# Tiles cut to the token group, and attention queries ahead of delta queries, in a two-layer streaming encoder

## The chip, the cores and the metric

The kernel runs on one core of a Trainium2 chip. The metric is the device time of one execution in microseconds. A kernel is timed in several runs; one further execution is profiled, and every row below comes from it.

## The reference

One inference step over two layers for 2048 prompt tokens and 8 x 16 sample tokens, model width 1024, float32. Cut to what matters:

```python
# layer 0
z = rms_norm(h) @ w_in        # a_q a_k a_v a_g | b_q b_k b_v b_g b_beta b_alpha
# mixer A: 8 query heads, 2 key heads of 64; a query block of 64 sees its chunk and two before
o_a = softmax([q k^T / 8 - slope * dist, sink]) v          # q, k rms-normed per head
# mixer B: 4 heads of 128; conv of width 4 + SiLU on q, k, v; l2-normed q, k
a_mat = tril(beta k k^T * decay, -1) + I                   # per block of tokens
u, w = solve(a_mat, [beta v, beta k exp(G)])
for each block:                                            # recurrence over blocks
    v_new = u - w S;  o = q_dec S + (q k^T * decay) v_new
    S = S * g_tot + k_dec^T v_new
y = h + concat(o_a * silu(a_g), rms_norm(o_b) * silu(b_g)) @ w_out
# layer 1: projection to u and gate, trailing means over 2/4/8/16 minus u, group map, gate, out
```

## The kernel before

The 2176 tokens are worked in four groups: group 0 has four prompt blocks of 128 and the sample block (n = 640 columns), groups 1 to 3 have four prompt blocks (n = 512). Within a group both layers run to the end. A projection is three matmuls for each of eight input tiles (high and low float32r halves: `XH`, `XL`, weights `wh`, `wl`). `proj_fm` (L682 to L684) puts features on partitions, `tok_major` (L1246 to L1248) tokens, `out_half` (L717 to L719) makes the output projections. Weights come in the order of `weight_plan`: in group 0 as float32, split on ScalarE, VectorE and GpSimd (L453, L457) and stored; in later groups loaded as split pairs (`wk` to `w`). Loads are asked for two blocks ahead on SyncE's queue.

The heads come in two pairs. For a pair, `b_keys` projects and convolves two delta keys and, for each head, `system` builds the decay table (`decay_logs`: L854 on VectorE, L855 on GpSimd; `decay_exp`: L864 on TensorE), takes k k^T (L898) and forms `L`. After the second head `b_chain` begins: `b_inverse` inverts the 32 x 32 diagonal blocks in 31 steps of two VectorE instructions (L963, L964), sends them through DRAM (`Xd`), and joins them with small matmuls (L990 to L1025); `b_recur` runs the recurrence (L1130, L1147, L1158), in group 0 also over the sample's states (L1177, L1181, L1202). `b_queries` projects and convolves two delta queries and two values (taps: L840; tanh product: L845). `a_queries` projects attention queries, normalises them and transposes them (L1348, L1354); then `a_attend` does the banded softmax (L1406, L1410, L1420, L1424, L1435 to L1437), in group 0 also for the sample (`unit_s`). `conv` evacuates PSUM with ScalarE into one of two `cb` buffers (L820). After both pairs come the gate projections, the two halves of the output projection, and layer 1.

The program text is put out by a planner. The projections call `tick` with their own price; `start`ed jobs (generators such as `b_chain`, `a_attend`, `rest` of a convolution) are stepped when their planned time has come. The framework then orders each engine's instructions by this priority as they become ready in its own model.

Large tiles live in 17 shared slots: eleven wide ones of 1280 elements per partition and six narrow ones of 1024. `slot` gives a tile of up to 1024 elements a narrow slot if one is free, else a wide one, in the order in which slots were dropped; a larger tile takes a wide one alone. With none free it steps the planner forward until one is dropped:

```python
        while True:
            if size <= SMALL and free_small:
                tag = free_small.pop(0)
                break
            if free_big:
                tag = free_big.pop(0)
                break
            if not progress():
```

A tile in a reused slot waits for the last reader of the tile that was there. Before the change the tiles of a pair (`kT`, `L`, `D`, queries, values `vb`, attention output `A`, gates, splits) have the width of group 0 (2 x 640 elements) in every group, and so has the decay table.

Of the kernel before, what the change touches and what calls it, by code (L numbers as in the profile page):

```python
# [90 lines left out]
def weight_plan():  # L91
# [5 lines left out]
    def add(part, cut):  # L97
        plan.append((part, cut))
# [27 lines left out]
    def queries(pr):  # L126
        for o in (0, 1024):
            for h in (2 * pr, 2 * pr + 1):
                add("B", cols("in", span(C_B + o + P * h, P)))
        c = np.concatenate([span(C_Q + 256 * g + P * pr, P) for g in range(2)])  # L130
        for k in range(2):
            add("A", k_half("in", 4 * k, c))

    for k in range(2):
        add("A", k_half("in", 4 * k, np.concatenate([span(C_K, 256), span(C_BA, 8)])))
    for pr in range(2):
        keys(pr)
        queries(pr)
    for pr in range(2):
# [86 lines left out]
def hybrid_kernel(  # L226
# [433 lines left out]
    def group(gix, norm_job):  # L660
# [189 lines left out]
        def decay_logs(h):  # L850

            r = slot([P, 2, NBMAX, P], F32R)
            rh, rl = r[:, 0], r[:, 1]
# [4 lines left out]
        def decay_exp(r, d):  # L858

            for b0, b1 in banks:  # L860
                pe = psum("sc")
                w = P * (b1 - b0)
                for i in range(2):
                    mm(pe[:, 0:w], m_le_r, r[:, i, b0:b1, :].rearrange("p c i -> p (c i)"),  # L864
                       start=(i == 0), stop=(i == 1))
                S.activation(d[:, P * b0:P * b1], pe[:, 0:w], AF.Exp)
            drop(r)
# [79 lines left out]
        def b_inverse(pr):  # L947
# [25 lines left out]
            XT = slot([P, 2 * NBMAX, P])  # L973
            G.memset(XT[:, 0:nh, :].rearrange("p c i -> p (c i)"), 0.0)
            XA = slot([P, 2 * NBMAX, 64])
# [9 lines left out]
            ta = slot([P, 2 * NBMAX, 32])  # L985
# [25 lines left out]
            ta = slot([64, 2 * NBMAX, 64])  # L1011
# [21 lines left out]
        def b_queries(pr):  # L1033
            kT, L, b1s, nb2s = st["k", pr]
            qas, ssqs = [], []
            vb = slot([P, 2, TMAX])
            st["q", pr] = (qas, ssqs, vb)

            def scores(e):
                qt, at = qas[e][:, 0, 0:n], qas[e][:, 1, 0:n]  # L1040
# [49 lines left out]
            for e in range(2):  # L1090
                qas.append(slot([P, 2, TMAX]))
                ssqs.append(buf([P, NBMAX], "ssq", 4))
                for _ in conv(2 * pr + e, qas[e][:, 0, 0:n], scores(e)):
                    pass
# [4 lines left out]
        def b_recur(pr):  # L1099
            kT, L, b1s, nb2s = st["k", pr]  # L1100
            qas, ssqs, vb = st["q", pr]
# [39 lines left out]
            for c in range(npb):  # L1141
                kds, rq, pv_ = [], [], []
                for e in range(2):
# [4 lines left out]
                    mm(p1[:, P:2 * P], qas[e][:, 0, tk], Sst[2 * pr + e], start=True, stop=True)  # L1148
# [6 lines left out]
                for e in range(2):  # L1155
# [3 lines left out]
                    mm(p2[:, P:2 * P], qas[e][:, 1, P * c:P * c + P], vn, start=True, stop=True)  # L1159
# [7 lines left out]
            if samp:  # L1167
                c = npb
                for e in range(2):
                    h = 2 * pr + e  # L1170
                    yield from room(4)
                    sin = slot([P, NBAT, P])
# [4 lines left out]
                    V.tensor_copy(kq[:, :, 1, :], qas[e][:, 0, srow].rearrange("p (b i) -> p b i", i=DSEQ))  # L1177
# [5 lines left out]
                    sx = slot([P, 2, NBAT, DSEQ])  # L1183
# [603 lines left out]
```

## Time and profile before

| | us |
|---|---|
| median of 3 runs | 1970.59 (1967.81 to 1972.84) |
| profiled execution | 1969.22 |
| its span | 1967.3 |
| TensorE busy | 1859.4 |
| VectorE busy | 1249.1 |

The span runs from the first to the last instruction of the profiled execution; the rest of its time, 1.9 us, lies around it. Busy times are sums over the engine's instructions; matmuls overlap each other, and the busy time counts a moment once. The granted clock is the mean over a stretch, as a share of 2.4 GHz.

### The profile page before, as it was taken

Reading aid. Unit: us, or ns where it says so; the run is one execution under the profiler, and the core shown is the slowest. Engines: PE = TensorE matmul, PEld = TensorE weight load, DVE = VectorE, ACT = ScalarE, POOL = GpSimd, SP = SyncE. Lnnn points to the kernel's source line nnn. Section 1 sums busy time; section 2 is a strip of 40 time slices with the busy share of each in tenths; the row PEclk is TensorE's granted clock in tenths of the full one; section 3 lists DMA queues with packets and bytes.
Section 4 is the critical chain, followed back from the end, with each engine's and each line's share of the span. In section 5 each row is a group of like instructions: output and inputs, shape, how many; then the busy total and the mean of one; then the engine's idle time right before and its main releaser. Section 6 shows DMA issues by size and latency. Waiting matters only on the chain.

```text
span 1967.3 us, 34503 instructions
## 1 busy us (share of the span) xinstructions
PE 1859.4 (95%) x12994; PEld 1689.5 (86%) x12994; DVE 1249.1 (63%) x3439; ACT 759.6 (39%) x1954; POOL 492.3 (25%) x628
## 2 busy tenths in 40 slices
PE   5989977999999999899999999999999999999999
PEld 4888876998999888789889888789889888889889
DVE  5897795546564586954445597954445587854343
ACT  5446445324332345551312346551322346451210
POOL 4561350332433331401101332301102332210000
PEclk8999997999999999999999999999999999999999
DMA  6343342565668542244457643344566543344454
GB/s 263 120 169 115 121 166 71 196 223 176 230 223 286 207 162 89 97 154 172 161 194 267 217 155 97 110 141 150 184 223 257 199 140 97 127 142 170 166 194 182
DMA packets 93875, 335.13 MB, mean 170 GB/s; under 512 B 35805, under 2 KB 44253, under 8 KB 64269
## 3 DMA queue, kind: packets, MB, share of 16 engines
q1 hardware_dynamic: 93708, 332.92, 48.5%
q8 instruction: 103, 1.69, 0.3%
q14 instruction: 64, 0.52, 0.1%
HBM read 254.31 MB, written 78.58 MB: 169 GB/s over the span
## 4 chain that ended last, share of the span: by engine, by line
PE 66%; DVE 15%; DMA 3%; issue 2%; ACT 2%; POOL 2%; SPq 0%; DVEq 0%; POOLq 0%; ACTq 0%
PE pj L682 11%; PE pj L683 10%; PE pj L684 10%; PE pj L717 6%; PE pj L718 6%; PE pj L719 6%; DVE A L964 3%; DVE tm L963 3%; DVE B L840 2%; DVE A L1354 1%; PE tp L1420 1%; DMA w<-wk 1%; PE sc L1735 1%; PE rc L1130 1%; PE sc L1736 1%
## 5 line engine op out<-in xcount | busy, mean ns | idle before, releaser
L682 PE MATMUL pj<-XH,w 128*128 128x512 f32 (+3 forms) x1488 | 541.6, 364 | 4.4 <-ACT cb L820 2.1
L684 PE MATMUL pj<-XH,w 128*128 128x512 f32 (+3 forms) x1488 | 534.1, 359 | 0.3 <-POOL w L457 0.3
L683 PE MATMUL pj<-XL,w 128*128 128x512 f32 (+3 forms) x1488 | 532.7, 358 | 0.0
L682 PEld LDWEIGHTS pj<-XH,w 128*128 128x128 f32 x1488 | 282.2, 190 | 36.0 <-ACT cb L820 3.2
L717 PE MATMUL pj<-w,B 128*128 128x256 f32 x1088 | 308.8, 284 | 2.6 <-DVE A L723 2.6
L684 PEld LDWEIGHTS pj<-XH,w 128*128 128x128 f32 x1488 | 282.2, 190 | 31.5 <-POOL w L457 0.6
L718 PE MATMUL pj<-w,B 128*128 128x256 f32 x1088 | 307.7, 283 | 1.5 <-POOL w L457 1.5
L683 PEld LDWEIGHTS pj<-XL,w 128*128 128x128 f32 x1488 | 282.4, 190 | 29.3 <-issue 0.7
L719 PE MATMUL pj<-w,B 128*128 128x256 f32 x1088 | 306.4, 282 | 0.0
L723 DVE TENSOR_TENSOR A<-pj,A 128x256 f32<-128x256 f32 x272 | 114.9, 422 | 179.5 <-PE pj L719 179.2
L717 PEld LDWEIGHTS pj<-w,B 128*128 128x128 f32 x1088 | 206.4, 190 | 3.7 <-DVE A L723 3.2
L718 PEld LDWEIGHTS pj<-w,B 128*128 128x128 f32 x1088 | 206.0, 189 | 1.9 <-POOL w L457 1.7
L719 PEld LDWEIGHTS pj<-w,B 128*128 128x128 f32 x1088 | 207.3, 191 | 0.0
L457 POOL TENSOR_TENSOR w<-wst,w 128x640 fp32r<-128x640 f32 (+3 forms) x60 | 111.1, 1854 | 127.2 <-ACT w L453 117.4
L840 DVE SCALAR_TENSOR_TENSOR B<-cb,taps,B 128x512 f32<-128x512 f32 x144 | 122.1, 851 | 11.7 <-ACT B L829 10.5
L1246 PE MATMUL pj<-w,XH 128*128 128x256 f32 (+1 forms) x368 | 108.9, 296 | 5.5 <-DMA w<-wk 5.5
L703 POOL TENSOR_TENSOR B<-B,B 128x512 fp32r<-128x512 f32 (+1 forms) x32 | 44.4, 1386 | 256.7 <-ACT B L702 139.5
L1248 PE MATMUL pj<-w,XL 128*128 128x256 f32 (+1 forms) x368 | 107.2, 291 | 0.0
L1247 PE MATMUL pj<-w,XH 128*128 128x256 f32 (+1 forms) x368 | 107.2, 291 | 0.0
L695 DVE SCALAR_TENSOR_TENSOR B<-B,pj 128x512 f32<-128x512 f32 (+1 forms) x60 | 36.3, 606 | 98.2 <-ACT B L694 97.8
L964 DVE TENSOR_TENSOR A<-A,tm 32x112 f32<-32x112 f32 (+27 forms) x248 | 95.2, 384 | 5.2
L963 DVE TENSOR_TENSOR tm<-A,A 32x112 f32<-32x112 f32 (+27 forms) x248 | 93.0, 375 | 7.1 <-DMA A<-Ld 2.0
(338 smaller groups left out, 3627.1 us busy)
## 6 DMA issues: line engine op xcount, KB each, us to landing
w<-wk SPq DMA_DIRECT2D x168, 1024.0 KB, 4.8
wk<-w SPq DMA_DIRECT2D x56, 1024.0 KB, 6.6
wst<-in_wts SPq DMA_DIRECT2D x56, 512.0 KB, 4.4
A<-in_x SPq DMA_DIRECT2D x31, 512.0 KB, 4.6
out_y<-A SPq DMA_DIRECT2D x17, 512.0 KB, 3.0
w<-wk SPq DMA_DIRECT2D x6, 1056.0 KB, 6.0
B<-in_xt SPq DMA_DIRECT2D x12, 512.0 KB, 4.7
w<-wk SPq DMA_DIRECT2D x12, 512.0 KB, 3.3
```

The lines of the kernel that those rows point to most:

```text
L457: eng.tensor_tensor(lo[:, a:b], st[:, a:b], f32(hi[:, a:b]), op=ALU.subtract)
L682: mm(pp[:, 0:w], wh[:, k, :], xh[:, k, t0:t1], start=(k == 0), stop=False)
L683: mm(pp[:, 0:w], wh[:, k, :], xl[:, k, t0:t1], start=False, stop=False)
L684: mm(pp[:, 0:w], wl[:, k, :], xh[:, k, t0:t1], start=False, stop=(k == KT - 1))
L717: mm(pp[:, 0:256], oh[:, tk], wh[:, k, :], start=(k == 0), stop=False)
L718: mm(pp[:, 0:256], oh[:, tk], wl[:, k, :], start=False, stop=False)
L719: mm(pp[:, 0:256], ol[:, tk], wh[:, k, :], start=False, stop=(k == 3))
L723: V.tensor_tensor(ysl, pp[:, 0:256], ysl, op=ALU.add)
L840: V.scalar_tensor_tensor(dst[:, 0:Tp], cb[:, j:j + Tp], taps[:, m, j:j + 1], dst[:, 0:Tp], op0=ALU.mult, op1=ALU.add)
L963: V.tensor_tensor(t3, bc(Lb[:, j + 1:32, j], w), bcm(Xb[:, j, 0:w], r), op=ALU.mult)
L964: V.tensor_tensor(Xb[:, j + 1:32, 0:w], Xb[:, j + 1:32, 0:w], t3, op=ALU.subtract)
L1246: mm(pp[:, 0:N], xh[:, k, tk], wh[:, k % 4, :], start=(k == 0), stop=False)
```

## The change

Shared tiles get the width of their group (`n` for `TMAX`, `nb` for `NBMAX`). The decay table becomes two tiles, one for each half. In the weight plan and in the program the attention queries of pair 0 come before its delta queries; pair 1 keeps its order. In group 0 the sample's attention queries are kept in the sample columns and the first 256 columns of the attention output tile, which is taken in `a_queries`. A delta query's two halves may take two narrow slots. The sample recurrence takes both its tiles at once when two slots are free; before it waited for four.

```diff
@@ weight_plan
+    def queries_a(pr):
         c = np.concatenate([span(C_Q + 256 * g + P * pr, P) for g in range(2)])
         for k in range(2):
             add("A", k_half("in", 4 * k, c))
     for pr in range(2):
         keys(pr)
+        if pr == 0:
+            queries_a(pr)
         queries(pr)
+        if pr:
+            queries_a(pr)
@@ split_pair; the same in b_keys, b_inverse, b_queries, gates, pooled
-            h = slot([P, 2, TMAX], F32R)
-            lo = slot([P, 2, TMAX], F32R)
+            h = slot([P, 2, n], F32R)
+            lo = slot([P, 2, n], F32R)
@@ decay_logs, decay_exp
-            r = slot([P, 2, NBMAX, P], F32R)
-            rh, rl = r[:, 0], r[:, 1]
+            r = [slot([P, nb, P], F32R) for _ in range(2)]
+            rh, rl = r
...
-            drop(r)
+            drop(*r)
@@ b_keys
-            kT = slot([P, 2, TMAX])
-            L = slot([P, 2 * NBMAX, P])
-            D = slot([P, 2, TMAX])
+            kT = slot([P, 2, n])
+            L = slot([P, 2 * nb, P])
+            D = slot([P, 2, n])
@@ b_queries
-                qas.append(slot([P, 2, TMAX]))
+                two = 2 * n > SMALL and not free_big and len(free_small) > 2
+                qs = [slot([P, n]) for _ in range(2)] if two else [slot([P, 2, n])]
+                qas.append([qs[0][:, 0, :], qs[0][:, 1, :]] if len(qs) == 1 else qs)
+                held_q.extend(qs)
@@ b_recur, sample
-                    yield from room(4)
-                    sin = slot([P, NBAT, P])
+                    yield from room(2)
+                    sin, sx = slot([P, NBAT, P]), slot([P, 2, NBAT, DSEQ])
...
-                    sx = slot([P, 2, NBAT, DSEQ])
@@ a_queries
-            qh = slot([P, 2, 2, 64]) if samp else None
-            st["qh", jp] = (qs, qh)
-            zs = [slot([P, 2, 4, 2, 64]) for _ in range(2)] + ([slot([P, 2, 2, 64])] if samp else [])
+            zs = [slot([P, 2, 4, 2, 64]) for _ in range(2)]
+            A = qh = None
+            if samp:
+                A = slot([P, 2, n])
+                qh = A[:, :, srow].rearrange("p c (j q) -> p c j q", q=64)
+                zs.append(A[:, 0, 0:256].rearrange("p (j g d) -> p j g d", j=2, d=64))
+            st["qh", jp] = (qs, qh, A)
@@ a_attend
-            A = slot([P, 2, TMAX])
+            A = A or slot([P, 2, n])
@@ group, the loop over pairs
+            if pr == 0:
+                a_queries(pr)
             b_queries(pr)
-            a_queries(pr)
+            if pr:
+                a_queries(pr)
```

## Rows read from the trace of the kernel before

**Rows 1.** The page's engine line: busy us, share of span, instructions.

```profile
PE 1859.4 (95%) x12994; PEld 1689.5 (86%) x12994; DVE 1249.1 (63%) x3439; ACT 759.6 (39%) x1954; POOL 492.3 (25%) x628
```

**Rows 2.** Stretches: us, busy us (instructions) by engine, clock, DMA, GB/s.

```profile
64.50:394.10 329.60, 285.92 (x2283) 267.37 (x2282) 254.90 (x766) 155.51 (x437) 116.05 (x121) 0.94 0.42 141
679.80:894.80 215.00, 206.63 (x1410) 178.03 (x1409) 165.80 (x522) 110.35 (x309) 52.44 (x77) 0.98 0.38 125
1118.90:1327.70 208.80, 202.18 (x1410) 174.40 (x1409) 164.43 (x519) 110.30 (x309) 51.78 (x77) 1.00 0.39 129
1554.40:1766.50 212.10, 205.43 (x1410) 176.96 (x1408) 165.40 (x522) 110.47 (x309) 50.93 (x73) 0.98 0.39 128
```

**Rows 3.** The same view, pooling layer of group 1.

```profile
983.60:1032.80 49.20, 49.20 (x218) 40.68 (x217) 20.97 (x30) 9.84 (x17) 4.16 (x10) 1.00 0.55 193
```

**Rows 4.** The same view: three parts in group 0, the last one's end.

```profile
64.50:151.80 87.30, 74.37 (x516) 72.88 (x515) 79.26 (x201) 38.93 (x100) 46.29 (x49) 0.94 0.49 162
151.80:231.60 79.80, 75.21 (x687) 68.34 (x686) 58.15 (x214) 46.17 (x138) 19.19 (x27) 1.00 0.36 128
231.60:334.60 103.00, 76.90 (x623) 70.83 (x622) 81.59 (x245) 44.16 (x131) 33.65 (x34) 0.87 0.33 113
...
282.50:334.60 52.10, 34.35 (x315) 31.66 (x313) 33.74 (x126) 20.24 (x62) 4.27 (x4) 0.74 0.30 103
```

**Rows 5.** The chain that ended last, 286 to 310 us: start, us, what.

```profile
296.83 1.06 DVE A L968
297.92 3.89 DMA Xd<-A
...
307.34 1.27 PE sc L990 x20
```

**Rows 6.** PE's waits in 64.5 to 394.1 us: us in total, times, longest.

```profile
PE sc L990 <- DMA B<-Xd: 15.6, 2, 14.9
PE tp L1348 <- DVE A L1354: 6.6, 3, 3.4
```

**Rows 7.** Stretches, as in rows 2: three parts in group 1.

```profile
679.80:749.50 69.70, 66.75 (x391) 57.34 (x390) 57.70 (x147) 29.50 (x71) 22.18 (x36) 1.00 0.45 147
749.50:826.80 77.30, 72.18 (x547) 63.42 (x546) 63.77 (x225) 45.74 (x139) 25.49 (x35) 0.93 0.25 86
826.80:894.80 68.00, 67.70 (x476) 57.28 (x475) 44.34 (x150) 35.11 (x100) 4.76 (x6) 1.00 0.44 147
```

**Rows 8.** VectorE's L845 by source (140 to 170 us) and by time.

```profile
L845 DVE SCALAR_TENSOR_TENSOR B<-t,B x1: 825/825/825, 152.1 to 152.1; 128x640 f32<-128x640 f32 x1
...
745.33 0.69 DVE L845 SCALAR_TENSOR_TENSOR B<-t,B 128x512 f32<-128x512 f32 x1 [0.70 <-ACT t L844]
```

**Rows 9.** GpSimd in order of time: start, us, instruction, [idle, releaser].

```profile
224.91 1.92 POOL L855 TENSOR_TENSOR B<-others,gl 128x640 fp32r<-128x640 f32 x1 [4.49 <-DVE t L1177]
...
781.35 1.16 POOL L855 TENSOR_TENSOR B<-others,gl 128x512 fp32r<-128x512 f32 x1 [4.79 <-PE rc L1147]
```

**Rows 10.** L964 by source, 250 to 300 and 790 to 850 us.

```profile
L964 DVE TENSOR_TENSOR A<-A,tm x31: 184/379/1793, 259.1 to 296.6; 40x31 f32<-40x31 f32 x2, 40x60 f32<-40x60 f32 x2, 40x87 f32<-40x87 f32 x2, 40x112 f32<-40x112 f32 x2
...
L964 DVE TENSOR_TENSOR A<-A,tm x31: 178/360/834, 803.7 to 841.1; 32x31 f32<-32x31 f32 x2, 32x60 f32<-32x60 f32 x2, 32x87 f32<-32x87 f32 x2, 32x112 f32<-32x112 f32 x2
```

**Rows 11.** The page's DMA issues: count, KB each, us to landing.

```profile
w<-wk SPq DMA_DIRECT2D x168, 1024.0 KB, 4.8
```

**Rows 12.** VectorE by line, 679.8 to 894.8 us: count, busy us, mean ns.

```profile
L1410 DVE CUSTOM_DVE_ANT_0 A<-sc,others 128x256 f32<-128x256 f32 x32 | 12.4, 420 | 3.3 <-PE sc L1407 3.1
L1424 DVE TENSOR_TENSOR pT<-tp,pT 128x512 fp32r<-128x512 f32 x16 | 10.9, 683 | 7.9 <-ACT pT L1423 7.9
...
L1410 DVE DVE_READ_ACCUMULATOR2_ANT mx<- 128x1 f32 x32 | 2.6, 82 | 0.0
...
L1380 DVE TENSOR_TENSOR es<-vec,mn 128x4 f32<-128x4 f32 x8 | 1.8, 229 | 0.1
...
L1373 DVE TENSOR_TENSOR mn<-mx,others 128x4 f32<-128x4 f32 x8 | 1.2, 155 | 0.1
```

More of the change, by code (lines that the diff above doesn't have):

```diff
@@ L972, in b_inverse @@
             drop(Xb, XbT)
-            XT = slot([P, 2 * NBMAX, P])
+            XT = slot([P, 2 * nb, P])
             G.memset(XT[:, 0:nh, :].rearrange("p c i -> p (c i)"), 0.0)
-            XA = slot([P, 2 * NBMAX, 64])
+            XA = slot([P, 2 * nb, 64])
             G.memset(XA[0:32, 0:nh, 32:64], 0.0)
@@ L983, in b_inverse @@
             yield XTW
-            ta = slot([P, 2 * NBMAX, 32])
+            ta = slot([P, 2 * nb, 32])
             for q in range(2):
@@ L1009, in b_inverse @@
             yield 1.2
-            ta = slot([64, 2 * NBMAX, 64])
+            ta = slot([64, 2 * nb, 64])
             for e in range(2):
@@ L1034, in b_queries @@
             kT, L, b1s, nb2s = st["k", pr]
-            qas, ssqs = [], []
-            vb = slot([P, 2, TMAX])
-            st["q", pr] = (qas, ssqs, vb)
+            qas, ssqs, held_q = [], [], []
+            vb = slot([P, 2, n])
+            st["q", pr] = (qas, ssqs, vb, held_q)
             def scores(e):
-                qt, at = qas[e][:, 0, 0:n], qas[e][:, 1, 0:n]
+                qt, at = qas[e]
                 sq = ssqs[e]
@@ L1090, in b_queries @@
             for e in range(2):
[L1091 removed]
+                two = 2 * n > SMALL and not free_big and len(free_small) > 2
+                qs = [slot([P, n]) for _ in range(2)] if two else [slot([P, 2, n])]
+                qas.append([qs[0][:, 0, :], qs[0][:, 1, :]] if len(qs) == 1 else qs)
+                held_q.extend(qs)
                 ssqs.append(buf([P, NBMAX], "ssq", 4))
[L1093 removed]
+                for _ in conv(2 * pr + e, qas[e][0], scores(e)):
                     pass
@@ L1195, in b_recur @@
                     yield 1.2
-                    mm(p2[:, P:2 * P], qas[e][:, 1, P * c:P * c + P], vn, start=True, stop=True)
+                    mm(p2[:, P:2 * P], qas[e][1][:, P * c:P * c + P], vn, start=True, stop=True)
                     output(e, c, p2, qs)
@@ L1565, in gates @@
             for _ in range(2):
-                gt = slot([P, 2, TMAX])
+                gt = slot([P, 2, n])
                 for e in range(2):
@@ L1660, in group @@
         for gi in range(4):
-            act = slot([P, 2, TMAX])
-            plh = slot([P, 2, TMAX], F32R)
-            pll = slot([P, 2, TMAX], F32R)
+            act = slot([P, 2, n])
+            plh = slot([P, 2, n], F32R)
+            pll = slot([P, 2, n], F32R)
             ubs, uss = [], []
@@ L1696, in pooled @@
                 def pooled(gi=gi, d=d, ut=ut, ub=ub, us=us, us2=us2, plh=plh, pll=pll):
-                    pl = slot([P, TMAX])
+                    pl = slot([P, n])
                     G.tensor_copy(hpool[:, ut, :], ub[:, Tp:Tp + HIST])
```

17 lines of the change are left out of this document (8 added, 9 removed).

## The prediction

> **What bounds the kernel now.** I read the page's engine line first. TensorE (PE) is busy 1859.4 us of a span of 1967.3, VectorE (DVE) 1249.1 [rows 1]; a saving must come out of PE's 108 us of idle time, out of PE time at the low clock, or out of matmuls that run one by one. Next I cut each of the four token groups at the stretch that the change touches, from the first matmul of the delta queries to the last of the gate projections. It is 329.60 us in group 0 and 215.00, 208.80 and 212.10 in the others; PE is idle 43.7, 8.4, 6.6 and 6.7 us there, at a mean clock of 0.94, 0.98, 1.00 and 0.98 [rows 2]. So 65 of the 108 idle microseconds lie here, two thirds of them in group 0. In the pooling layer PE is busy 49.20 of 49.20 us [rows 3]; nothing is to be had there.
>
> The Trainium skill ("Trainium Kernel Development and Optimization", Best Practices) says that slack is judged by the busy share of weight loads, not of matmuls. Here that is 86%, which would leave 278 us. The trace does not agree: in a stretch that streams without a gap weight loads are busy only 40.68 of 49.20 us, 83% [rows 3]. I keep to idle time and clock.
>
> Then I cut the stretches finer, to see which engine ends the waits. Group 0 has three parts. In 64.5 to 151.8 us DVE is busy 79.26 of 87.30; in 151.8 to 231.6 it is idle 21.6 us; in 231.6 to 334.6 PE is idle 26.1 us at a mean clock of 0.87, and the bottom is 282.5 to 334.6, where PE works 34.35 of 52.10 us at 0.74, a mix of its levels 1.2 and 2.4 GHz [rows 4]. The chain of waits shows what PE waits for there: the copy that ends the 31-step inverse on DVE (L968), its way through DRAM, then the first matmul that reads it (L990) [rows 5]; that one wait is 14.9 us [rows 6]. Group 1 is a mild copy: DVE 57.70 of 69.70 us, then PE idle 5.1 us at 0.93, then PE full [rows 7].
>
> Why is that inverse late? It needs the second pair's decay table, built by L854 and L855. The keys of that pair's second head are ready at 152.1 us in group 0 and 745.3 in group 1 [rows 8]. L855 runs at 224.91 and 781.35, and what it waits for is not its data: in group 0 it is L1177, the first pair's last sample head, in group 1 L1147, the first pair's last recurrence chunk [rows 9]. Both stand where the first pair's key tile is read for the last time (L1176, L1177 copy the sample's keys and queries). By the code, all eleven wide slots are then held, the table asks for a wide one, and the planner runs the recurrence forward until its key tile comes free. The second pair's inverse (31 steps of L964) therefore starts at 259.1 us in group 0 and at 803.7 in group 1 [rows 10]. The second pair's delta chain is strung behind the first pair's by a buffer, 72.8 and 36.0 us after its keys.
>
> **The change part by part.** *Widths.* In groups 1 to 3 n is 512, so a pair tile is 1024 elements and fits a narrow slot; the decay table becomes two tiles of 640 or 512 elements, narrow in every group. All 17 slots then serve, and by my count of tiles the table finds two free in all four groups. No instruction is added or changes its size. What goes is the wait of rows 9. What is late next is the keys' own L898 and then DVE.
>
> *Attention queries first, pair 0.* The same two weights and matmuls move ahead of four projections. SP's loads move with them: the two blocks pass the four delta blocks in the queue. A 1 MB block lands in 4.8 us [rows 11], a projection of 24 matmuls at 49.20/218 = 0.226 us streams 5.4 us [rows 3], and blocks are asked for two ahead; I take nothing, hidden by the projection before it; uncovered it would be at most two loads, 9.6 us a group. POOL and ACT only see the splits of group 0 in another order. What matters is that attention of pair 0 becomes ready four projections earlier and meets the first pair's inverse on DVE. Its DVE work in group 1, two pairs together, is 12.4 + 10.9 + 2.6 for L1410 and L1424, and 6.9 for five small lines: 32.8, so 16.4 us a pair [rows 12]. DVE's idle time in the first part is 87.3 - 79.3 = 8.0 us in group 0 [rows 4] and 12.0 in group 1 [rows 7]. If all of it lands there, 8.4 and 4.4 us do not fit. DVE runs in order, so queued behind it are the conv taps (L840) that free PE's evacuation buffers. Lower bound nothing (PE runs other projections meanwhile), upper bound the overflow in full; DVE is the nearest row to full there, so I take it in full.
>
> *Sample queries in the output tile; room(2) for room(4); split query tiles.* Group 0 holds two slots fewer and the first copy of attention's output waits for four sample transposes that stand before it anyway. Zero, hidden by attention's own softmax; if that cover were gone, one attention unit late, 16.4/4 = 4.1 us once.
>
> *The gain, group 0.* The chain can come forward by as much as DVE has room before it, the 21.6 us idle in 151.8 to 231.6 [rows 4]. PE then gets up to 21.6 of the 26.1 idle us after 231.6 back, and of the low clock, (1 - 0.87) x 76.9 = 10.0 us, the same share, 8.3. That is 29.9, less the overflow 8.4: **21.5 us**. Bounds: nothing, if the recurrence of the sample still ends last, and the whole stretch's idle time and clock, 43.7 + 0.06 x 285.9 = 60.9 us.
>
> *The gain, groups 1 to 3.* In 749.5 to 826.8 PE is idle 5.1 us, and its clock costs (1 - 0.93) x 72.2 = 5.1 [rows 7]. DVE, rid of 16.4 us there, has 47.4 left in 77.3, so I take both: 10.2, less 4.4: **5.8 us**, three times 17.4. Bounds: nothing, and all idle time and clock of the three stretches [rows 2]: 8.4 + 4.1, 6.6 + 0, 6.7 + 4.1, together 29.9 us.
>
> Sum: 21.5 + 17.4 = 38.9 us off the profiled execution's 1969.22: 1930.3. That execution lies 0.07% under the median of the runs, 1970.59, so I forecast **1930 us**.
>
> **The rivals.** *Only group 0 gains.* In groups 1 to 3 PE's idle time is small and group 1 works 749.5 to 826.8 at 93% although the table waits. For it: the stretches of groups 1 to 3 differ by 6.2 us with equal work [rows 2], as much as I expect. Against it: 36 us of lateness. Then 21.5 - 3 x 4.4 = 8.3 us, 1961.
>
> *It doesn't do what it says.* The table gets its slots, but DVE is so full (81.59 of 103.00 us around the second inverse [rows 4]) that the rounds start when they did, or the planner runs out of slots elsewhere in group 0, where pair tiles stay wide. Against it: the 21.6 us of idle DVE just before. 1969.
>
> *Slower: DVE is overfull in the first part.* The first inverse, the taps and attention of pair 0 now want DVE together. It decides where DVE's busy share of the first part reaches 100% and the second part gives nothing back; then 8.4 + 3 x 4.4 = 21.6 us are lost, 1991. For it: DVE stands at 91% there in group 0. Against it: what is moved leaves the second part. The Trainium skill speaks for this rival ("TensorE: Matmul & The Clock Gate", on engine queue depths): ACT and DVE run strictly in order, so a round of the inverse cannot pass an attention reduction placed before it. The trace agrees with that order: PE's transposes (L1348) wait up to 3.4 us for L1354 behind other DVE work [rows 6].
>
> **How the numbers follow.** Forecast 0.62, only group 0 0.13, no change 0.11, slower 0.14. The likeliest's own range is 1890 to 1950: all bounds at once would be 1969 - 60.9 - 29.9 = 1878, which needs every gap closed. The range goes from 1885 to 1978, which leaves out the end of the slower case and the last of the gain, some 0.17. A measurement of this kernel tells a change from none at about 0.3%, 6 us. Faster takes the forecast and most of the second case, 0.73; same is no change and the rest of it, 0.12; slower 0.15.
>
> **What would show it.** Right: L855 of the second pair no longer released by L1147 or L1177; L964's third run of group 0 starting about 20 us earlier against the stage's start; no wait of 14.9 us at L990; the clock of that stretch near 1.00; group 0's stretch shorter by about 20 us and the others' by about 6. DVE's share of the first parts rises to 95% or more. Wrong: first parts longer by more than the second ones shrink, new waits of PE on L820 or L840, or a table that waits for another tile's last reader.

## The result, and the profile after

The changed kernel takes 1949.83 us (median of 4 runs, 1948.46 to 1951.19) against 1969.2 (4 runs, 1963.92 to 1972.84) for the kernel before: a ratio of 0.9904, 95% interval 0.9879 to 0.9928. It is faster by 19.4 us, 1%: clear of the noise, and half of the 38.9 that the forecast summed up. The profiled execution took 1951.19 us, its span 1949.2. The page's engine line answers to [rows 1]: VectorE is busy 30.6 us less with the same 3439 instructions, TensorE 3.6 us more.

```profile
PE 1863.0 (96%) x12994; PEld 1687.7 (87%) x12994; DVE 1218.5 (63%) x3439; ACT 758.5 (39%) x1954; POOL 496.2 (25%) x628
```

The lines of the table and of the inverse are 6 higher than before (L855 is now L861, L964 is L970); L1348 and L1354 became L1362 and L1368. The stretches of [rows 2], from the first query matmul to the last of the gates:

```profile
64.40:376.00 311.60, 285.04 (x2283) 266.19 (x2283) 239.76 (x766) 152.91 (x437) 120.33 (x122) 0.96 0.45 149
660.30:870.30 210.00, 204.05 (x1409) 173.46 (x1408) 160.66 (x521) 110.70 (x308) 57.64 (x81) 1.00 0.38 128
1097.10:1307.60 210.50, 205.32 (x1409) 175.11 (x1408) 161.55 (x521) 110.12 (x308) 55.33 (x81) 0.98 0.38 128
1533.80:1748.40 214.60, 207.99 (x1409) 177.98 (x1408) 161.16 (x521) 110.90 (x308) 55.42 (x77) 0.98 0.38 127
...
64.40:151.80 87.40, 77.80 (x551) 74.91 (x550) 77.25 (x235) 47.12 (x130) 41.23 (x48) 0.96 0.41 138
151.80:230.40 78.60, 74.15 (x671) 70.45 (x672) 62.35 (x222) 40.53 (x128) 25.81 (x33) 0.93 0.42 134
230.40:314.30 83.90, 74.30 (x608) 66.54 (x607) 62.45 (x199) 39.98 (x112) 36.20 (x29) 0.96 0.46 160
281.20:314.30 33.10, 31.50 (x323) 27.89 (x322) 21.12 (x89) 20.61 (x64) 3.48 (x2) 1.00 0.41 142
660.30:730.00 69.70, 69.03 (x429) 58.65 (x428) 60.80 (x197) 47.06 (x130) 21.49 (x33) 1.00 0.37 126
...
774.50:801.90 27.40, 22.48 (x162) 20.06 (x160) 26.03 (x63) 10.96 (x28) 17.07 (x20) 1.00 0.31 116
...
1211.60:1239.60 28.00, 24.12 (x162) 22.18 (x160) 26.02 (x66) 11.07 (x28) 14.65 (x19) 0.88 0.32 114
```

Group 0 is 18.0 us shorter; groups 1 to 3 differ by -5.0, +1.7 and +2.5, together -0.8. So the gain of the span, 18.1 us, is group 0's alone. The four rows from 64.40:151.80 on answer to [rows 4]: the first part is as long as before with VectorE at 88%, not 95%; the third went from 103.00 to 83.90 us and its clock from 0.87 to 0.96, the bottom's to 1.00. In group 1 the first part is again 69.70 us, as in [rows 7]; the idle time of TensorE has moved to 774.5 to 801.9, where it is busy 22.48 of 27.40 us and VectorE 26.03. VectorE's share of the first part is 87% there (60.80 of 69.70), against the 95% that the forecast named as a sign.

The wait at L990 [rows 6] is gone. In group 0 a wait of 3.3 us for an evacuation buffer (L826, L820 before; the longest for it was 1.1 us) has come, one of the forecast's signs of being wrong. TensorE's waits (us in total, times, longest), first in group 0, then in group 1:

```profile
PE tp L1362 <- POOL B L1279: 5.6, 3, 3.4
PE pj L688 <- ACT cb L826: 3.3, 1, 3.3
...
PE tp L1362 <- DVE A L1368: 3.8, 2, 3.5
```

The table of the second pair (GpSimd in order of time, as in [rows 9]; two heads in group 0, two in group 1), and then VectorE's L970 by source, as in [rows 10]:

```profile
170.49 1.26 POOL L861 TENSOR_TENSOR A<-others,gl 128x640 fp32r<-128x640 f32 x1
...
190.40 1.26 POOL L861 TENSOR_TENSOR A<-others,gl 128x640 fp32r<-128x640 f32 x1 [7.55 <-PE tp L1478]
...
749.22 1.05 POOL L861 TENSOR_TENSOR A<-others,gl 128x512 fp32r<-128x512 f32 x1 [3.60 <-PE sc L1022]
751.26 1.32 POOL L861 TENSOR_TENSOR A<-others,gl 128x512 fp32r<-128x512 f32 x1 [1.00 <-PE sc L870]
```

```profile
L970 DVE TENSOR_TENSOR A<-A,tm x31: 183/375/1283, 216.5 to 266.4; 40x31 f32<-40x31 f32 x2, 40x60 f32<-40x60 f32 x2, 40x87 f32<-40x87 f32 x2, 40x112 f32<-40x112 f32 x2
...
L970 DVE TENSOR_TENSOR A<-A,tm x31: 169/357/1156, 772.1 to 810.6; 32x31 f32<-32x31 f32 x2, 32x60 f32<-32x60 f32 x2, 32x87 f32<-32x87 f32 x2, 32x112 f32<-32x112 f32 x2
```

None of these tables waits for the first pair's recurrence any more. Some still come right behind the last reader of another tile, which the forecast had named as a sign of being wrong: L1478 transposes the sample's attention scores, L1022 joins the first pair's inverse. They are early all the same: the second heads' tables run 126.0 us (group 0) and 91.0 us (group 1) after the group's first query, where it was 160.4 and 101.6. Counted from the group's first query, the second inverse starts at 152.1 us in group 0 (194.6 before) and at 111.8 in group 1 (123.9 before). The forecast had expected about 20 us in group 0 and got 42.5. The chain is 12 us earlier in group 1 and the stage gained 5 us there, nothing in groups 2 and 3. That was to be explained.

### The profile page after: what moved, and what is told of

It is laid out like the page before. It is cut to its first block, busy times and chain, and to the rows that moved or that the text cites. A ratio compares the mean times of both kernels' runs of the same rounds, so it can differ in the third digit from the quotient of the medians.

```text
span 1949.2 us, 34495 instructions
## 1 busy us (share of the span) xinstructions
PE 1863.0 (96%) x12994; PEld 1687.7 (87%) x12994; DVE 1218.5 (63%) x3439; ACT 758.5 (39%) x1954; POOL 496.2 (25%) x628
## 4 chain that ended last, share of the span: by engine, by line
PE 76%; DVE 14%; issue 3%; DMA 2%; POOL 2%; ACT 2%; SPq 0%; DVEq 0%; POOLq 0%; ACTq 0%
PE pj L688 12%; PE pj L690 12%; PE pj L689 12%; PE pj L723 6%; PE pj L724 6%; PE pj L725 6%; DVE tm L969 3%; DVE A L970 2%; PE pj L1255 1%; PE pj L1257 1%; PE pj L1256 1%; PE tp L1434 1%; PE rc L1140 1%; DVE B L846 1%; DMA w<-wk 1%
## 5 line engine op out<-in xcount | busy, mean ns | idle before, releaser
L725 PE MATMUL pj<-w,B 128*128 128x256 f32 x864 | 243.5, 282 | 0.0
L723 PE MATMUL pj<-w,B 128*128 128x256 f32 x768 | 217.8, 284 | 1.4 <-DVE A L729 1.4
L724 PE MATMUL pj<-w,B 128*128 128x256 f32 x768 | 217.3, 283 | 1.5 <-POOL w L463 1.5
L725 PEld LDWEIGHTS pj<-w,B 128*128 128x128 f32 x864 | 164.3, 190 | 0.0
L463 POOL TENSOR_TENSOR w<-wst,w 128x640 fp32r<-128x640 f32 (+3 forms) x60 | 112.1, 1870 | 145.2 <-ACT w L459 136.3
L723 PEld LDWEIGHTS pj<-w,B 128*128 128x128 f32 x768 | 146.5, 191 | 1.9 <-DVE A L729 1.6
L724 PEld LDWEIGHTS pj<-w,B 128*128 128x128 f32 x768 | 145.5, 189 | 1.7 <-POOL w L463 1.7
L729 DVE TENSOR_TENSOR B<-pj,B 128x256 f32<-128x256 f32 x144 | 60.8, 422 | 100.4 <-PE pj L725 99.5
L729 DVE TENSOR_TENSOR A<-pj,A 128x256 f32<-128x256 f32 x128 | 54.0, 422 | 79.6 <-PE pj L725 79.3
L723 PE MATMUL pj<-w,A 128*128 128x256 f32 x320 | 91.5, 286 | 0.0
L724 PE MATMUL pj<-w,A 128*128 128x256 f32 x320 | 90.8, 284 | 0.0
L459 ACT CAST w<-wst 128x1024 fp32r<-128x1024 f32 (+1 forms) x60 | 61.2, 1019 | 58.0 <-PE pj L725 44.2
L701 DVE SCALAR_TENSOR_TENSOR A<-A,pj 128x512 f32<-128x512 f32 x36 | 24.7, 686 | 90.9 <-ACT A L700 90.9
```

Of the source, the lines that this page charges most:

```text
L459: S.copy(hi, st)
L463: eng.tensor_tensor(lo[:, a:b], st[:, a:b], f32(hi[:, a:b]), op=ALU.subtract)
L723: mm(pp[:, 0:256], oh[:, tk], wh[:, k, :], start=(k == 0), stop=False)
L724: mm(pp[:, 0:256], oh[:, tk], wl[:, k, :], start=False, stop=False)
L725: mm(pp[:, 0:256], ol[:, tk], wh[:, k, :], start=False, stop=(k == 3))
L729: V.tensor_tensor(ysl, pp[:, 0:256], ysl, op=ALU.add)
```

## The experiments

One measure serves for all: the stretch from the first query matmul to the first matmul of the pooling layer (the stretch above with the output projection), read by the view of stretches. The ratio is to the kernel before, which ran on the same chip each time; where it is missing below the first row there was one execution, and the time stands alone (the kernel before took 1973.84 us beside the first two of these, 1962.6 beside the next three, 1969.02 beside the last four). Stretches come from one profiled execution each; where kernels share a group's code, as after, e_g0 and e_p1 in group 0, they agree within 0.5 us.

| kernel | time, us | ratio (95%) | group 0 | mean of groups 1 to 3 |
|---|---|---|---|---|
| before | 1969.2 | | 390.7 | 261.2 |
| after | 1949.83 | 0.9904 (0.9879 to 0.9928) | 373.0 | 260.6 |
| e_order | 1975.09 | 1.0036 (1.0023 to 1.0049) | 376.8 | 268.8 |
| e_width | 1991.77 | 1.0118 (1.0099 to 1.0137) | 386.7 | 269.6 |
| e_split | 1971.73 | 1.0027 (1.001 to 1.0044) | 386.3 | 264.0 |
| e_ow | 1950.34 | 0.9915 (0.989 to 0.994) | 371.0 | 260.3 |
| e_g0 | 1979.68 | 1.0054 (1.0035 to 1.0072) | 373.4 | 268.7 |
| e_p1 | 1987.22 | 1.0103 (1.008 to 1.0126) | 373.5 | 272.4 |
| e_both | 1938.56 | 0.9856 (0.9836 to 0.9875) | 373.5 | 256.8 |
| e_few_before | 1898.95 | | 351.0 | 251.7 |
| e_few_after | 1906.57 | | 354.9 | 251.2 |
| e_few_width | 1913.73 | | 356.4 | 252.0 |
| e_few_order | 1906.86 | | 348.4 | 253.9 |
| e_few1_after | 1918.09 | | 358.9 | 254.8 |
| e_load_before | 1951.91 | | 367.2 | 262.5 |
| e_late_before | 1944.12 | | 385.4 | 255.3 |
| e_load_after | 1939.35 | | 366.4 | 258.5 |
| e_late_after | 1943.86 | | 367.1 | 259.4 |

### One part alone

**e_order**: the new order in the weight plan and in the loop over pairs, nothing else.

```diff
+            if pr == 0:
+                a_queries(pr)
             b_queries(pr)
-            a_queries(pr)
+            if pr:
+                a_queries(pr)
```

> The kernel before with the order of pair 0 alone: attention queries first, tiles and decay table as wide as before. If group 0's gain of 18 us comes from the decay table's slot, the table still waits for the first pair's last readers, group 0's stretch stays near 330 us and the time near 1969. If it comes from the order, because attention is out of the way sooner, the stretch is near 312 us and the time near 1950.

The order alone gives 13.9 of group 0's 17.7 us and costs a mean of 7.6 in each later group, so neither expected time came. The table still waits for the slot, released by the same copy as in [rows 9] in group 0 (L1183 was L1177) and by the recurrence in group 1 (GpSimd by time):

```profile
210.72 1.93 POOL L861 TENSOR_TENSOR B<-others,gl 128x640 fp32r<-128x640 f32 x1 [3.19 <-DVE t L1183]
...
776.29 1.40 POOL L861 TENSOR_TENSOR B<-others,gl 128x512 fp32r<-128x512 f32 x1 [1.94 <-PE rc L1153]
```

In group 0 that is 146.0 us after the first query, where it was 160.4: the order brings the first pair's recurrence 14 us forward and the table with it. In group 1 it is 112.1, where it was 101.6: there the order delays the first pair, and the second chain's recurrence runs into the output projection. That projection, 48.7 us long in group 1 before (263.7 - 215.00), takes 71.60 here, while the stretch ahead of it is shorter (199.5 us against 215.00):

```profile
863.70:935.30 71.60, 65.01 (x497) 61.63 (x496) 36.87 (x105) 20.04 (x53) 12.29 (x11) 0.95 0.35 119
```

**e_width**: the hunks with `n`, `nb` and the two-tile table; old order, the sample's tiles as before.

```diff
-            r = slot([P, 2, NBMAX, P], F32R)
+            r = [slot([P, nb, P], F32R) for _ in range(2)]
...
-            kT = slot([P, 2, TMAX])
+            kT = slot([P, 2, n])
```

> The kernel before with the tile widths alone: pair tiles of the group's width, decay table as two tiles, old order of the queries, sample queries in their own tiles. If the slot is the cause, the second table no longer waits for the first pair's recurrence in any group, group 0 is 18 us shorter and the time is near 1951. If the order is the cause, 1969. In groups 1 to 3 the table is free in either case; the forecast's gain there (5.8 us a group) would show without the order's overflow as up to 10 us a group, the theory that nothing is to be had there says 0.

The slot wait is gone, and the kernel is slower by 1.2%, which neither cause had foreseen. Group 0's second table runs at 193.0 us, 32 us earlier than before, and the group is 4.0 us shorter. In group 1 the second inverse starts at 791.8, 6 us earlier against the stage's start than before, and takes 47.5 us where it took 37.4 [rows 10]; it shares VectorE with more attention than before (13 of its large instructions in that time, 8 before). The stretch grows by 7.9 us.

```profile
L964 DVE TENSOR_TENSOR A<-A,tm x31: 172/362/1390, 791.8 to 839.3; 32x31 f32<-32x31 f32 x2, 32x60 f32<-32x60 f32 x2, 32x87 f32<-32x87 f32 x2, 32x112 f32<-32x112 f32 x2
```

**e_split**: the kernel before with the two-tile table alone (the first two diff lines above, with its two readers).

> The kernel before with nothing but its decay table made of two tiles; all pair tiles keep the width of group 0. Theory (the early table alone does what the widths did): group 0 comes down by 4 us to 387, and in groups 1 to 3 the second pair's inverse starts under the first pair's attention and each stretch grows by some 8 us, to 270: 1990. Rival (the widths cost, through other slots that are reused in another order, not the table): group 0 387, groups 1 to 3 unchanged at 261, 1965. The second pair's table shows which applies: before 192 us after the group's first query in neither, one or all groups.

Group 0 comes out as with all the widths, 386.3. Groups 1 to 3 lose 2.8 us, a third of what the widths cost: neither of the two expectations (nothing, 8 us) holds. The mean is made of -0.6, +7.0 and +1.9 us, although the second inverse starts earlier and lasts 45 to 48 us in all three groups. What carries the rest of the widths' cost is not shown.

**e_ow**: e_width and e_order together, without the sample queries in the output tile, the two narrow tiles for a delta query and `room(2)`.

> Widths, the table in two tiles and the order of the first pair; the sample's attention queries keep their own two tiles, a delta query keeps one wide tile and the sample recurrence waits for four slots, as before the change. In groups 1 to 3 this is the changed kernel. Theory (the sample's parts carry nothing, as the prediction costed them): group 0 from the first query to the pooling layer takes 373 us as with the change, groups 1 to 3 a mean of 260.6, the time is 1950. Rival (they carry the step from the order alone to the whole change in group 0, 376.8 to 373.0 us): 377 us in group 0, 1954. A third case, that without them group 0 runs out of slots while its queries wait and loses what the order gave: 385 us or more, 1962 or more.

This is the changed kernel's time. The sample's parts carry nothing that these runs can tell, as the prediction costed them. And the parts are not additive: in groups 1 to 3 the order costs 7.6, the widths 8.4, the two together -0.9.

### The order of one pair

**e_g0**: the changed kernel, with the new order in group 0 alone.

```diff
-            if pr == 0:
+            first = gix == pr == 0
+            if first:
                 a_queries(pr)
             b_queries(pr)
-            if pr:
+            if not first:
                 a_queries(pr)
```

> The changed kernel with the new order in group 0 alone; groups 1 to 3 keep the new tiles and take delta queries first again. If the order costs in groups 1 to 3 what the tiles give there, their stretches shrink by 5 us each and the time is near 1935. If neither matters there, it stays within 4 us of the changed kernel's 1950.

Both expectations missed. Groups 1 to 3 go to 268.7: with the widths in place, the order there is worth 8.1 us a group. It pays for what the widths cost, no more.

**e_p1**: as e_g0, but in groups 1 to 3 the second pair has its attention queries first (`first = (pr == 1) == (gix > 0)`).

> The changed kernel; group 0 as changed, in groups 1 to 3 the first pair has its delta queries first as before and the second pair its attention queries first. The mean stretch of groups 1 to 3 from the first query to the pooling layer is 268.8 us with neither pair turned, 260.6 with the first and 256.8 with both. Theory A (the two orders add): 268.8 - 3.8 = 265.0, the time 1968. Theory B (what costs is the second inverse under the second pair's query transposes, and moving those transposes away is enough): 258 to 261, 1945 to 1953. Theory C (the first pair's order is what matters, the second's helps only behind it): 268 to 270, 1978.

All three theories missed: 272.4 us, the worst of all. The trace shows lateness here. The matmul that reads the inverted blocks (L1000, before L990) waits up to 5.9 us in group 1 and up to 7.6 in group 2. The second pair's tables run 105 to 109 us after the first query, where e_g0 has them at 87 to 88. That too little is left to lie over the chain's end is a reading; no run tested it. TensorE's waits in group 2:

```profile
PE sc L1000 <- DMA A<-Xd: 8.5, 2, 7.6
```

**e_both**: the changed kernel, attention queries first in both pairs.

```diff
-            if pr == 0:
-                a_queries(pr)
+            a_queries(pr)
             b_queries(pr)
-            if pr:
-                a_queries(pr)
```

> The changed kernel with attention queries first in both pairs. In groups 1 to 3 PE's idle time that is left stands at the second pair's query transposes, which wait 3.4 to 3.6 us for VectorE under the second inverse. If that pile-up is what ate the gain, the waits go and each of the groups is some 4 us shorter: near 1938. If VectorE only piles up elsewhere (second inverse against the second pair's taps), 1950 or above.

The first expectation held, and the kernel beats both others: 0.9856 of the time before. Group 0 keeps its gain, and groups 1 to 3 come to 258.4, 255.8 and 256.3 us, at a clock of 1.00 and 5.8 to 3.6 us of idle TensorE time, group 1 here:

```profile
664.30:922.70 258.40, 252.59 (x1814) 221.31 (x1813) 182.34 (x577) 119.72 (x329) 63.09 (x86) 1.00 0.39 134
```

The second pair's query transposes now come before its inverse, and transposes waiting for VectorE to empty them are not among TensorE's waits in group 1; the longest wait of all is 1.5 us.

### Without the inverse's steps

**e_few_before** and **e_few_after**: the kernels before and after with the first 3 of 31 steps.

```diff
             for j in range(31):
+                if j < 3:
...
                 yield INV
```

> The kernel before, of the 31 steps of each inverse only the first 3 done (28 steps of two VectorE instructions are left out, some 35 us of VectorE work for a pair, 70 for a group, 280 in all; all else stays). Theory (TensorE is full in groups 1 to 3, a late second inverse costs little there): groups 1 to 3 shrink by at most their idle TensorE time, 8 us each, to 253 to 258; group 0, where the inverse ended TensorE's longest wait, loses 25 to 40 us. Together 1910 to 1930. Rival (the second inverse sets the end in every group): groups 1 to 3 shrink by 20 us or more each, to 241 or less, and the time falls under 1890.

> The changed kernel with the same 28 of 31 steps of each inverse left out. Theory: groups 1 to 3 end at the same 253 to 258 us as in the kernel before without the steps, since both are then bound by TensorE's work alone; group 0 shrinks less than it does in the kernel before, by 10 to 25 us, since the change has already taken its longest wait; the two kernels without the steps differ by less than 8 us. Rival (the change in groups 1 to 3 is held back by its inverse on VectorE): it shrinks there by 10 us or more per group and ends 20 us or more under the kernel before without the steps.

Groups 1 to 3 come to 251.7 and 251.2 us, a little under the 253 to 258 expected of both, and the first kernel's time lies under its 1910 to 1930; neither rival's number came. That is near the floor that TensorE's own work sets, busy 248.37 of 251.60 us at full clock in group 1 of the first:

```profile
64.60:415.60 351.00, 335.30 (x2790) 319.88 (x2789) 236.82 (x735) 174.42 (x471) 129.96 (x134) 0.99 0.50 168
638.40:890.00 251.60, 248.37 (x1814) 222.21 (x1812) 150.83 (x465) 120.61 (x329) 57.61 (x85) 1.00 0.41 137
```

So the 28 steps hold 9.5 us a group there, and the change took 0.6 of them. In group 0 the steps were worth 39.7 us before and are worth 18.1 after. With the steps gone the change gains nothing: 1906.57 us against 1898.95.

**e_few_width** and **e_few_order**: the same edit in e_width and e_order.

> The widths and the two-tile table alone (old order), with 28 of the 31 steps of each inverse left out. Theory (what the widths cost in groups 1 to 3 is the second inverse sharing VectorE with the first pair's attention): the mean stretch of groups 1 to 3 falls from 269.6 to the 251 to 253 us of the kernels before and after without the steps. Rival (the widths cost through slots reused in another order, so that tiles wait for each other): the stretch stays 5 us or more above that, 257 or more.

> The order alone (old widths, table in one tile), with the same 28 steps of each inverse left out. Theory A (the order costs through the end of the second inverse, which comes late): groups 1 to 3 fall from 268.9 to 251 to 254 us. Theory B (the late second table itself, held by the slot, makes the second chain late with or without the steps, and the end of the recurrence finds no projection to lie under): they stay at 257 or more, since the table still waits for the first pair's recurrence.

252.0 and 253.9 us. Without the steps the four variants, which lay at 260.6 to 269.6, lie within 2.7 us. What sets them apart in groups 1 to 3 goes with the steps. For the order, theory A holds: the table still waits for its slot in that kernel, and it costs at most 2.7 us.

**e_few1_after**: the 28 steps left out of the second pair's inverse alone.

```diff
+                if j < 3 or pr == 0:
```

> The changed kernel with the 28 steps left out of the second pair's inverse alone; the first pair's is whole. Theory (what is left of idle TensorE time in groups 1 to 3 of the changed kernel belongs to the second inverse on VectorE): groups 1 to 3 come to 251 to 254 us, nearly all of the 9 us that leaving out both gave, and group 0 to about 358. Rival (it belongs to the first inverse, which now shares the first part with the first pair's attention): they stay at 257 or more.

254.8 us, just over the theory's range: of the 9.4 us that both inverses hold in groups 1 to 3, leaving out the second's steps gives 5.8, and in group 0 14.1 of 18.1.

### Load or lateness

The steps hold two things, the time that the chain needs and VectorE's load. Two edits on top of e_few_before and e_few_after take them apart.

**e_load_before, e_load_after**: the load without the lateness, in a job that nothing waits for.

```diff
+        def load_only(NB32):
+            for j in range(3, 31):
...
+                V.tensor_tensor(t3, bc(m_gt[0:NB32, j + 1:32], w), bcm(m_gt[0:NB32, 0:w], r), op=ALU.mult)
+                V.tensor_tensor(t3, t3, bcm(m_gt[0:NB32, 0:w], r), op=ALU.subtract)
+                yield INV
...
+                if j == 3:
+                    start(load_only(NB32))
```

**e_late_before, e_late_after**: the lateness without the load, on ScalarE.

```diff
+                    else:
+                        S.copy(t3, Xb[:, j + 1:32, 0:w])
+                        S.copy(Xb[:, j + 1:32, 0:w], t3)
```

> The kernel before with the same edit as in the changed kernel: the chain short, VectorE's load kept in a job that nothing waits for. In groups 1 to 3 theory A (load) gives 257 or more against 261.3 in the kernel before, theory B (lateness) 251 to 254. In group 0, where the second inverse ended a wait of 14.9 us, the lateness should count for most: 355 to 365 of 390.7 us.

> The kernel before with the 28 steps as ScalarE copies: the chain late, VectorE free. In groups 1 to 3 theory A (load) gives 251 to 255 us, theory B (lateness) 257 or more. In group 0 the lateness stays: 375 or more of 390.7 us.

In groups 1 to 3 theory A, the load, holds on both sides: 262.5 us with the load and a short chain (261.2 in the kernel before), 255.3 with the chain late and the load gone, 0.3 over its range. In group 0 it is the other way round: a short chain gives 23.5 us although the load is there (367.2, just over the 355 to 365 expected), taking the load off 5.3.

Neither edit does its half purely. In groups 1 to 3 the copy that ends the second chain still stands far behind its last step in VectorE's order (36 us in group 1 of e_load_before), so the joining matmuls of the second pair, 174.9 us after the first query in group 1 before, come at 157.0 in e_load_before and, a little earlier than before too, at 166.2 in e_late_before. The kernel with the earlier chain has the longer stretch, so lateness cannot be what sets them apart there. The first of these matmuls in time, before, e_load_before, e_late_before:

```profile
854.74 0.69 PE L990 MATMUL sc<-B,B 32*32 32x32 f32 x16
813.42 0.69 PE L1002 MATMUL sc<-B,B 32*32 32x32 f32 x16
839.02 0.69 PE L995 MATMUL sc<-B,B 32*32 32x32 f32 x16
```

The stretches of groups 0 and 1, first e_load_before, then e_late_before:

```profile
65.50:432.70 367.20, 345.62 (x2790) 328.51 (x2789) 276.43 (x847) 174.92 (x471) 135.37 (x134) 0.96 0.47 160
656.40:919.20 262.80, 252.25 (x1813) 224.51 (x1812) 187.51 (x577) 119.29 (x329) 62.05 (x85) 0.98 0.39 131
```

```profile
65.00:450.40 385.40, 348.61 (x2792) 328.28 (x2791) 245.96 (x735) 204.47 (x583) 129.64 (x135) 0.95 0.45 153
672.80:927.70 254.90, 249.94 (x1813) 222.57 (x1812) 150.50 (x465) 147.55 (x441) 57.34 (x85) 1.00 0.40 135
```

TensorE's largest wait in group 1 of e_load_before is the changed kernel's: L1360 and L1366 are the query transposes and the VectorE instruction that empties them. An earlier chain with its load in place makes this wait longer: in the kernel before it came to 2.8 us in group 1, at most 1.4 at once.

```profile
PE tp L1360 <- DVE A L1366: 5.0, 3, 3.3
```

> The changed kernel with 28 of the 31 steps of each inverse left out, and in their place the same number of VectorE instructions of the same sizes in a job of its own that nothing waits for (it reads a constant and writes a scratch tile). VectorE's load is as in the changed kernel, the chain is short. Theory A (the load on VectorE holds groups 1 to 3 back, the chain's lateness does not): they stay near the changed kernel's mean of 260.6 us, 257 or more. Theory B (the lateness holds them back): 251 to 254. Group 0: by A 365 or more, by B 355 to 360.

> The changed kernel with 28 of the 31 steps of each inverse done as two ScalarE copies each, one behind the other on the same tile, in place of the two VectorE instructions (the elimination itself is left out). The chain takes about as long, VectorE is rid of its load, ScalarE has 56 more instructions a chain. Theory A (load on VectorE): groups 1 to 3 come to 251 to 255 us, if ScalarE, busy 120 us of 259 there, hides the copies. Theory B (lateness): they stay at 257 or more. Group 0: by A 365 or less, by B 368 or more.

With the load and a short chain the changed kernel keeps 258.5 of 260.6 us, within theory A's bound. e_late_after gives 259.4, the number of theory B, which here stands against the load. It does not decide: the gates' stretch in group 1, 81.80 us in the changed kernel, is 77.80, while the second pair's before it, where steps of both inverses now lie on ScalarE beside the attention (busy 60.99 us, 41.00 in the changed kernel), grows from 76.40 to 82.20:

```profile
707.80:790.00 82.20, 79.16 (x575) 68.95 (x573) 56.01 (x172) 60.99 (x192) 24.26 (x38) 0.98 0.29 90
790.00:867.80 77.80, 76.24 (x523) 64.08 (x522) 41.88 (x140) 41.92 (x127) 12.73 (x18) 1.00 0.45 153
```

By these rows ScalarE did not hide the copies there, which was the condition of that expectation. In group 0 both give 366 to 367, 6 us under the changed kernel: theory A's number for the first, between the two theories for the second.

## Why the forecast was wrong

The step that failed is "The gain, groups 1 to 3": 10.2 us a group from idle time and clock, less 4.4. The stretches came out 5.0 us shorter, 1.7 and 2.5 us longer. The step took the 5.1 us of idle time in 749.5 to 826.8 us [rows 7], and the low clock beside it, for the price of a late chain. The trace of the kernel before already says otherwise. There 4.2 of the 5.1 us are waits of the query transposes (L1348) for GpSimd and VectorE, and none is for the chain; in the whole stretch of group 1 the wait for the chain (L990) is 1.5 us, in the next two groups 1.0 and 1.6. TensorE's waits in 679.8 to 894.8 us:

```profile
PE tp L1348 <- DVE A L1354: 2.8, 3, 1.4
PE tp L1348 <- POOL A L1270: 2.8, 2, 2.0
PE sc L990 <- DMA B<-Xd: 1.5, 1, 1.5
```

The forecast had looked up who ends TensorE's waits in group 0 alone [rows 6] and called group 1 a mild copy of it. e_load_before shows the same by a run: a chain 18 us earlier at its joining matmuls is worth nothing there as long as VectorE carries the steps. And the step gave VectorE room by an average, 47.4 us of work in 77.3. Where the inverse went there was no room. VectorE in the changed kernel, in order of time, and the transposes on TensorE:

```profile
789.46 0.41 DVE L970 TENSOR_TENSOR A<-A,tm 32x255 f32<-32x255 f32 x1
789.90 0.49 DVE L1368 SCALAR_TENSOR_TENSOR A<-tp,gq,A 64x256 fp32r<-64x256 f32 x1
790.42 0.84 DVE L969 TENSOR_TENSOR tm<-A,A 32x256 f32<-32x256 f32 x1
791.30 0.72 DVE L970 TENSOR_TENSOR A<-A,tm 32x256 f32<-32x256 f32 x1
792.04 0.49 DVE L1368 SCALAR_TENSOR_TENSOR A<-tp,gq,A 64x256 fp32r<-64x256 f32 x1
```

```profile
792.68 0.63 PE L1362 MATMUL tp<-first,B 128*128 128x128 f32 x4 [3.46 <-DVE A L1368]
```

Each L1368 stands behind a round of the inverse, and the matmul that it releases has waited 3.46 us. The slower rival had named this order of work on VectorE and this very wait; it had it in the first part, and it came at the second pair's queries. So in groups 1 to 3 the change moved TensorE's wait more than it removed it.

**Overflow.** 8.4 us in group 0 and 4.4 in each other group were charged for attention in the first part. Nothing came: 87.40 and 69.70 us, as before, with VectorE busy 2.0 us less in group 0 and 3.1 more in group 1, where 16.4 more were feared. This mis-sized term hid part of the failed one; without it the sum would have been 29.9 + 3 x 10.2 = 60.5 us.

**Group 0.** 21.5 us forecast, 18.0 measured: the size is near by luck, since a gross gain of 29.9 that was too high met a charge of 8.4 that never came. A late chain was a real cost there (e_load_before, 23.5 us), but the slot is not its main part. The table alone gives 4.0 to 4.4 us (e_width, e_split), the order alone 13.9; the prediction had put the order down as a cost. The earlier start does not tell the two apart: the second inverse starts 176.1 us after the first query in e_order and 176.4 in e_width (194.6 before). But it runs for 37.3 us in the first and 48.6 in the second. And e_both shows that group 0 can gain without an earlier chain: its second table runs 161.3 us after the first query (160.4 before), the inverse's last step 236.7 (232.1 before), and the group is 17.2 us shorter all the same. The rows, e_order's inverse, e_width's, then e_both's with its table:

```profile
L970 DVE TENSOR_TENSOR A<-A,tm x31: 183/366/1134, 240.8 to 278.1; 40x31 f32<-40x31 f32 x2, 40x60 f32<-40x60 f32 x2, 40x87 f32<-40x87 f32 x2, 40x112 f32<-40x112 f32 x2
L964 DVE TENSOR_TENSOR A<-A,tm x31: 183/356/566, 241.1 to 289.7; 40x31 f32<-40x31 f32 x2, 40x60 f32<-40x60 f32 x2, 40x87 f32<-40x87 f32 x2, 40x112 f32<-40x112 f32 x2
L967 DVE TENSOR_TENSOR A<-A,tm x31: 183/362/1759, 249.8 to 301.4; 40x31 f32<-40x31 f32 x2, 40x60 f32<-40x60 f32 x2, 40x87 f32<-40x87 f32 x2, 40x112 f32<-40x112 f32 x2
226.04 1.26 POOL L858 TENSOR_TENSOR A<-others,gl 128x640 fp32r<-128x640 f32 x1
```

What differs in e_both is the work that TensorE has beside the chain. From the second inverse's first step to the joining matmul it is idle 19.9 of 46.2 us before, 6.6 of 64.9 in e_both:

```profile
259.10:305.30 46.20, 26.31 (x180) 24.88 (x179) 36.81 (x84) 12.60 (x26) 15.99 (x15) 0.86 0.52 182
249.80:314.70 64.90, 58.34 (x424) 54.28 (x423) 54.44 (x163) 38.59 (x114) 17.57 (x19) 0.97 0.38 121
```

So the wait of 14.9 us goes when the chain comes earlier, or when other work lies over it; which of the two gave how much of the change's 18.0 us stays open. Even with both parts of the change, the first-query-to-pooling stretch keeps 18.1 us that the steps hold (e_few_after).

**Sample parts**, zero: right (e_ow). **The signs.** The table no longer released by the recurrence, no long wait at the joining matmul, the clock back: right in group 0. VectorE at 95% in the first parts: wrong.

**The rivals.** "Only group 0 gains" is what happened in groups 1 to 3; its 1961 was too high by its three charges of 4.4, without which it gives 1969.2 - 21.5 = 1947.7. "It doesn't do what it says" did not happen: the second inverses start 42.5 and 12.1 us earlier.

Open is which of the inverse's neighbours on VectorE cost what in e_width's 8.4 us: that they go with the steps is shown (e_few_width), their split is only read from the trace. e_split's 2.8 us were not taken further, nor was e_late_after's 259.4.

## What to carry to other kernels

Before pricing a wait, look up in each stretch who ends it; what holds in one group need not hold in the next. When a wait is taken away, ask what the work that now starts earlier will run beside, on the engine that it occupies, and look at that engine's busy share in that stretch and not over a longer part. To price lateness, make the late work short and leave its load in place; to price load, do the reverse, and read in the trace how far each kernel really moved the chain. Here the two gave one answer in group 0 and the opposite one in groups 1 to 3. And a change in two parts is not the sum of its parts: each alone was slower, together they were 1% faster.

## What the runs showed of the hardware

**VectorE's busy time holds time in which it is blocked.** Its 847 instructions of group 0's stretch to the pooling layer were busy 286.09 us before and 270.99 after; with the old order it is 282 to 286 in every kernel with all steps, with the new one 266 to 279. The taps (L840, then L846, 128x512) by source in that stretch show where some of it went (about 3.5 of the 15.1 us; the rest is spread over many lines), minimum, median and maximum in ns, before and after:

```profile
L840 DVE SCALAR_TENSOR_TENSOR B<-cb,taps,B x35: 623/742/1914, 64.7 to 254.6; 128x512 f32<-128x512 f32 x35
```

```profile
L846 DVE SCALAR_TENSOR_TENSOR B<-cb,taps,B x32: 732/736/751, 63.8 to 253.7; 128x512 f32<-128x512 f32 x32
L846 DVE SCALAR_TENSOR_TENSOR A<-cb,taps,A x3: 737/746/1779, 212.4 to 215.9; 128x512 f32<-128x512 f32 x3
```

The longest of them before, in order of time, GpSimd's instruction and VectorE's:

```profile
145.50 1.94 POOL L457 TENSOR_TENSOR w<-wst,w 128x640 fp32r<-128x640 f32 x1
...
146.07 2.70 DVE L840 SCALAR_TENSOR_TENSOR B<-cb,taps,B 128x512 f32<-128x512 f32 x2
```

Two taps take 2.70 us, not 2 x 0.74: they start 1.37 us before GpSimd's weight split ends and come out 1.2 us late. In the whole kernel before, 20 of the 144 taps of this shape start under a GpSimd instruction and end 0.54 to 0.55 us after it, so that they take 0.88 to 1.91 us; others run under one at their usual length. The Trainium skill ("SBUF — State Buffer", SBUF: two separate sides) says that a VectorE instruction with two SBUF inputs and a GpSimd instruction that reads SBUF contend for a shared port pair, which the first to start holds for its whole instruction. By that rule the taps would wait for the split's end, which agrees with the 1.2 us. So a sum of VectorE durations taken from one order of the work does not carry over to another.

**The granted clock differs at the same wait.** The wait at L1362 is 3.5 us at its longest in group 1 and 3.4 in group 2, with 162 matmuls around it in both. The granted clock of that stretch, a mix of 1.2 and 2.4 GHz where it is under 1, is 1.00 in group 1 and 0.88 in group 2 (774.50 and 1211.60 above), and TensorE is busy 22.48 and 24.12 us. Why one dropped and the other did not, these runs do not show.
